# An encoder layer on one core: TensorE and the DMA queue of the mixer in source order

## The chip, the cores and the metric

The kernel runs on one core of a Trainium2 chip. The metric is device time of one execution in microseconds, lower is better. The kernel before took 881.35 us (median of three runs, 881.19 to 881.5). A core has TensorE (PE in the profile: matmuls and transposes, with PEld for its weight loads), VectorE (DVE), ScalarE (ACT), GpSimd (POOL) and SyncE (SP, which here only starts DMA transfers). Each takes its instructions from its own queue, one after the other, and they meet at semaphores.

## The reference

One layer of an encoder: half a SwiGLU step, a mixer, another half SwiGLU step, a final norm. Sequence 512, width 1024, float32 throughout.

```python
x = x + 0.5 * swiglu(rms_norm(x, ffn1_norm), ffn1_w_gate, ffn1_w_up, ffn1_w_down)
h = rms_norm(x, mix_norm)
u = h @ w_in                        # 512 fourier | 8x64 q | 2x64 k | 2x64 v
f_out = fourier_mixer(u[..., :512], fnet_w, fnet_b)
a_out = gqa_attention(u[..., 512:1024], u[..., 1024:1152], u[..., 1152:], q_norm, k_norm)
x = x + jnp.concatenate([f_out, a_out], axis=-1) @ w_out
x = x + 0.5 * swiglu(rms_norm(x, ffn2_norm), ffn2_w_gate, ffn2_w_up, ffn2_w_down)
return rms_norm(x, final_norm)
```

The Fourier half takes, for each of four groups of 128 channels, the real part of a two-dimensional Fourier transform over positions and channels, and then a 128 by 128 linear map. The attention half has eight query heads on two key/value heads; queries and keys get an RMS norm and a rotary turn in two axes, and the softmax is over all 512 positions.

## The kernel before

Every product is made of three passes: each operand is split into a high part, rounded to PE's fast float32 format, and a low part, the remainder. `product` (L100 to L103) issues high by high (L101), high by low (L102) and low by high (L103). So each weight block is loaded as it is (`raw_tile`, L85 to L87, a ring of three buffers), cast to its high part by ACT (L96; by VectorE at L94 for the two blocks f0 and f1), and its low part is made by VectorE (`lows`, L72). The parts stand in slots that are handed round; a slot is free when the last matmul that reads it is done.

The two FFNs (`ffn`) are recorded under `in_order()`: in them PE and SP keep the order of the source. The mixer between them is not. There a scheduler, at build time, orders the instructions of all engines by its own estimate of their times. The source order of the mixer is only its starting point.

The mixer, in the order of its source: k, the first query block q0 and v are projected (`project`; eight steps of one `product` each). `rope` turns k and q: it makes the squares for the norm (sq), a copy with the halves swapped (sw), and three VectorE steps with the tables cos and sin. For q1 to q3 the swap is made by four DMA transfers on SP's queue out of a copy (own). `heads` (pq, sc) sums the squares on PE, and VectorE, GpSimd (a power) and VectorE again turn them into a factor. `keys` (kp) transposes the factors of the keys (kw) and scales k with them; `value_stacks` (vp) transposes v.

Then the loop `attend` runs over 32 scores (t: query block, b: head group, c: block of 128 queries). At step n it issues the score n (s, L777 and L778; then mx on VectorE: a maximum, L781, and its scaling, L782; then the exponent e on ACT, L784), the transpose of the probabilities of step n - 4 (pt, L790; cast to ph on ACT, low part pl on VectorE), and the product with the values of step n - 6 (o, L809 and L810). A transpose of block kc reads all four exponents of its group, so the first of a group follows the group's last score at a distance of one step. Between the steps, in shares of a cost, stand the entries of the list `fill`: the projections q1 to q3, the Fourier half's projection (`fproject`, f, from the weight blocks f0 to f3), the fold of its linear map (`fold`, map), the transform over positions (`positions`, dft) and over channels (`channels`, pc and psn). After the loop come eight blocks of the output projection (out), each of eight products, four with the Fourier half (mh, ml) and four with attention (qa, qb), and the second FFN.

Loads stand where the cast of their block stands: `project` and `fload` call `weights`, which issues the load and the cast. cos and sin are loaded at the top of the mixer; the transform's tables chan, pos and odd come by GpSimd's queue.

Of the kernel before, what the change touches and what calls it, by code (L numbers as in the profile page):

```python
# [13 lines left out]
P = 128  # L14
S = 512
D = 1024
KD = D // P
# [7 lines left out]
FILL_LEAD = 0.1  # L25
# [18 lines left out]
def encoder(ctx, tc, A, out):  # L44
    nc = tc.nc
# [7 lines left out]
    def bank(name):  # L53
        return pp.tile([P, S], F32, tag="bank", name=name)
# [9 lines left out]
    def in_order():  # L64
        return tc.manual_schedule(engines={mybir.EngineType.PE, mybir.EngineType.SP})

    def run(steps):
        for _, f, a in steps:
            f(*a)
# [12 lines left out]
    def weight_slots():  # L82
        return (slot().rearrange("p (a b) -> p a b", b=P) for _ in range(2))

    def raw_tile(src, name, n=KD):  # L85
        raw = wp.tile([P, KD, P], F32, tag="raw", name=f"raw_{name}")
        nc.sync.dma_start(out=raw[:, :n, :], in_=src)  # L87
        return raw

    def weights(src, name, n=KD, raw=None):  # L90
        raw = raw or raw_tile(src, name, n)
        hi, lo = weight_slots()
        if name in HI_DVE:
            nc.vector.tensor_copy(hi[:, :n, :], raw[:, :n, :])  # L94
        else:
            nc.scalar.copy(hi[:, :n, :], raw[:, :n, :])  # L96
        lows(lo[:, :n, :], raw[:, :n, :], hi[:, :n, :])
        return hi, lo

    def product(ps, whi, wlo, mhi, mlo, first, last):  # L100
        nc.tensor.matmul(ps, whi, mhi, start=first, stop=False)  # L101
        nc.tensor.matmul(ps, whi, mlo, start=False, stop=False)  # L102
        nc.tensor.matmul(ps, wlo, mhi, start=False, stop=last)  # L103

    class Norm:
# [29 lines left out]
        def add(self, k):  # L135
            self.scale(k)
            self.sums(k)
# [360 lines left out]
    raws = [wp.tile([P, 4, 2, P], F32, tag="raw", name=f"raw_first{i}") for i in range(KH)]  # L498
# [45 lines left out]


    n2 = Norm(2)
    with tc.tile_pool(name="mix", bufs=1) as mp, tc.tile_pool(name="mixt", bufs=1) as mt:

        more = mp.tile([P, 2, KD * P], F32R, name="more")
        more = [more[:, i, :] for i in range(2)]  # L550
# [3 lines left out]
            return mt.tile([P, S], F32, tag="t", bufs=9, name=name)  # L554

        cos = mp.tile([P, S], F32, name="cos")
        nc.sync.dma_start(out=cos, in_=A["cos"])
        sin = mp.tile([P, S], F32, name="sin")
        nc.sync.dma_start(out=sin, in_=A["sin"])
        chan = mp.tile([P, 4, P], F32R, name="chan")  # L560
        pos = mp.tile([P, 2, 2, 514], F32R, name="pos")
        odd = mp.tile([1, 258], F32R, name="odd")

        sc = mp.tile([P, 4, 10], F32, name="sc")

        def project(c, name):

            whi, wlo = weights(A["wins"][c], f"in{c}")
            ps = bank(name)
            banks[name] = ps  # L570

            def step(k):
                product(ps, whi[:, k, :], wlo[:, k, :], hh[k], hl[k], k == 0, k == KD - 1)

            return [(0.65, step, (k,)) for k in range(KD)]
# [100 lines left out]
        fws = {}  # L676

        def fload(i):
            if i == "fw":
                fws[i] = [  # L680
                    w[:, :4, :].rearrange("p a b -> p (a b)")
                    for w in weights(A["fw"].rearrange("p (a b) -> p a b", b=P), "fw", 4)
                ]
                return
            src = A["winf"][i].rearrange("p a (b c) -> p (a b) c", c=P)
            if i == 3 and i not in fws:
                fws[i] = raw_tile(src, "f3")
                return
            h, l = weights(src, f"f{i}", raw=fws.get(i))
            fws[i] = [w.rearrange("p (a b) c -> p a (b c)", a=4) for w in (h, l)]  # L690

        def fproject(h, c, i):
# [25 lines left out]
        mh, ml = ([e[g // 2][g % 2].rearrange("p a b -> p (a b)") for g in range(4)] for e in (eh, el))  # L718
# [68 lines left out]
        def turn(t, b, kc):  # L787
            pt = bank(f"pt{t}{b}{kc}")
            for c in range(4):
                nc.tensor.transpose(pt[:, c * P : (c + 1) * P], prob[t, b, c][:, kc * P : (kc + 1) * P], ident)  # L790
            ph = mt.tile([P, S], F32R, tag="ph", bufs=3, name=f"ph{t}{b}{kc}")
            pl = mt.tile([P, S], F32R, tag="pl", bufs=3, name=f"pl{t}{b}{kc}")
            nc.scalar.copy(ph, pt)
            lows(pl, pt, ph)
            parts[t, b, kc] = ph, pl
            if b == 1 and kc == 0:

                zw = tp.tile([P, 4, 2, HD], F32, tag="wide", bufs=1, name=f"zw{t}")
                nc.vector.reciprocal(zs[t], zs[t])
                nc.gpsimd.tensor_copy(zw, zs[t].unsqueeze(3).to_broadcast([P, 4, 2, HD]))  # L800
                zs[t] = zw

        def values(t, b, kc):
            if kc == 0:
                outs[t, b] = bank(f"o{t}{b}")
            po = outs[t, b]
            ph, pl = parts[t, b, kc]
            w = vst[:, b, kc].rearrange("p a e -> p (a e)")
            nc.tensor.matmul(po, w, ph, start=kc == 0, stop=False)  # L809
            nc.tensor.matmul(po, w, pl, start=False, stop=kc == 3)  # L810
            if kc == 3:
                own = slice(b * HD, (b + 1) * HD)
                if b == 0:
                    pair[t] = tp.tile([P, S], F32, tag="u", name=f"oo{t}")
                o = pair[t]
                nc.scalar.copy(o[own], po[HD:P])
                nc.vector.tensor_tensor(out=o[own], in0=po[0:HD], in1=o[own], op=ALU.add)
                if b == 1:
                    zp = bank(f"zp{t}")
                    for c in range(4):  # L820
                        nc.tensor.transpose(
                            zp[:, c * P : (c + 1) * P], zs[t][:, c].rearrange("p a b -> p (a b)"), ident
                        )
                    nc.vector.tensor_tensor(out=o, in0=zp, in1=o, op=ALU.mult)
                    nc.scalar.copy(qa[t], o)
                    lows(qb[t], o, qa[t])


        scale = HD**-0.5
        key = project(0, "k")  # L830
        q0 = project(1, "q0")
        run(key)
        rope("k", qkg[:, 1:2])
        n1.column([n1.acc])
        val = project(5, "v")
        run(q0[:5])
        key_scales()
        run(q0[5:])
# [1 line left out]
        query(0)  # L840
        for t, n in ((chan, "chan"), (pos, "pos"), (odd, "odd")):
            nc.gpsimd.dma_start(out=t, in_=A[n])
        q1 = project(2, "q1")
        run(val[:2])
        keys()
# [12 lines left out]
        fill = []  # L858
# [4 lines left out]
        for t in (1, 2, 3):  # L863
            for k in range(KD):
                add(step, t, k, cost=0.65)
                if k == 0 and t < 3:
                    add(load, t + 1)
                if t == 3 and k in (0, 4):
                    add(fload, k // 4)
                if k == 3:  # L870
                    add(*((value_stacks,) if t == 1 else (heads, f"q{t - 1}", t, scale)), cost=0.3)
            add(query, t)
        for h in range(2):
            for n, c in enumerate((0, 2, 1, 3)):
                for i in range(2):
                    add(fproject, h, c, i, cost=1.3)
                    if h == 0 and n == 3 and i == 0:
                        add(fload, 3)
                if h == 0 and n == 0:
                    add(heads, "q3", 4, scale)  # L880
                if h == 0 and n in (1, 2):
                    add(fload, n + 1)
                if h == 1 and n == 0:
                    add(fload, "fw")
        add(fold, cost=1.3)
# [7 lines left out]
        def attend(n):  # L893
            def at(m):
                return m // 8, m // 4 % 2, m % 4

            if n < 32:
                scores(*at(n))
            if 4 <= n < 36:
                turn(*at(n - 4))  # L900
            if n >= 6:
                values(*at(n - 6))

        whole = sum(c for c, _, _ in fill)
        done = 0.0
        for n in range(38):
            while fill and done < whole * (FILL_LEAD + (1 - FILL_LEAD) * n / 38):
                done += fill[0][0]
                run([fill.pop(0)])
            attend(n)  # L910
        run(fill)

        mh, ml = mh + [qa[t] for t in range(4)], ml + [qb[t] for t in range(4)]
        for d in range(KD):
            whi, wlo = weights(A["wo"][d], f"o{d}")
            ps = bank(f"out{d}")
            for k in range(KD):
                product(ps, whi[:, k, :], wlo[:, k, :], mh[k], ml[k], k == 0, k == KD - 1)
            nc.vector.tensor_tensor(out=x[d], in0=ps, in1=x[d], op=ALU.add)
            n2.add(d)  # L920

# [5 lines left out]
    ready = (3, 4, 5)  # L927
# [158 lines left out]
```

## Time and profile before

| what | value |
|---|---|
| median of three runs | 881.35 us (881.19 to 881.5) |
| the profiled execution | 882.0 us |
| its span, from the first to the last instruction | 880.1 us |
| first FFN on PE, to the last down projection | to 353.2 us |
| mixer on PE | 353.2 to 523.6 us |
| granted clock of PE | 1.00 in the mixer, 0.995 over the span |
| DMA in the span | 85.55 MB, mean 97 GB/s |

The profile describes one execution. Its times are counted from the span's start. A row of the kind "L72 DVE ... pl<-pt,ph" names the source line, the engine, and what is written from what; lines are often those of a helper. A row of waits names who waited for whom, then the sum in us, the number of waits and the longest. A row of a timeline has the start and the length in us; what stands in brackets is the idle time of the engine before it and what ended that. A row of stretches has, for PE, PEld, DVE, ACT and POOL in turn, the busy time and the number of instructions, then PE's clock, the busy share of the DMA engines and GB/s. A DMA queue's row has packets, MB and the share of 16 DMA engines that its packets took. Busy time of PE is pipelined: a matmul's shown end is modelled and lies after the start of the next one.

### The profile page before, as it was taken

What the parts mean: (1) busy time and instruction counts of PE and PEld (TensorE: products, weight loads), DVE (VectorE), ACT (ScalarE), POOL (GpSimd) and SP (SyncE); (2) the same over time, 40 slices, a digit from 0 to 9 for tenths busy, and PEclk for the clock granted to TensorE, in tenths of its full rate; (3) what the DMA queues carried; (4) which work ended last, traced back from release to release, by engine and by line L of the source; (5) the groups of instructions that cost most, each with busy time, mean ns of one, the idle gap of its engine ahead of it and who ended that gap; (6) DMA issues with size and microseconds to landing.
All of it is one profiled execution on the core that took longest, in us unless ns stands there. A gap on an engine that the chain in (4) does not pass through costs nothing.

```text
span 880.1 us, 13432 instructions
## 1 busy us (share of the span) xinstructions
PE 863.1 (98%) x5334; PEld 766.7 (87%) x5334; DVE 640.4 (73%) x1003; ACT 451.0 (51%) x746; POOL 24.7 (3%) x32
## 2 busy tenths in 40 slices
PE   8999999999999999999999999999999999999995
PEld 5888999889989988888888888889998999889985
DVE  7798788459757837699888558977975688469444
ACT  7454466226525634677775436535652365327432
POOL 0000000000000000211000000000000000000002
PEclk9999999999999999999999999999999999999998
DMA  7324232333243113521110223242224232322212
GB/s 245 112 67 164 98 118 86 99 116 104 69 141 114 55 36 108 204 83 37 50 48 25 94 67 127 75 141 97 108 79 140 88 119 69 105 110 85 73 36 96
DMA packets 29150, 85.55 MB, mean 97 GB/s; under 512 B 3488, under 2 KB 6560, under 8 KB 28960
## 3 DMA queue, kind: packets, MB, share of 16 engines
q1 hardware_dynamic: 28560, 83.37, 28.1%
q0 software_dynamic: 384, 1.32, 0.5%
q8 instruction: 41, 0.67, 0.3%
q14 instruction: 21, 0.17, 0.1%
q10 hardware_dynamic: 144, 0.02, 0.0%
HBM read 81.81 MB, written 2.10 MB: 95 GB/s over the span
## 4 chain that ended last, share of the span: by engine, by line
PE 56%; issue 39%; DVE 2%; ACT 2%; DMA 1%; POOL 0%; SPq 0%; POOLq 0%; ACTq 0%; DVEq 0%
PE r L304 10%; PE q L304 5%; PE dn L103 4%; PE dn L101 4%; PE dn L102 4%; PE p L304 3%; PE gu L103 2%; PE gu L102 2%; PE gu L101 2%; PE out L101 2%; PE out L103 2%; PE out L102 2%; PE pt L790 1%; PE q L101 1%; PE q L102 1%
## 5 line engine op out<-in xcount | busy, mean ns | idle before, releaser
L304 PE MATMUL r<-rt,ring 128*128 128x256 f32 x1584 | 207.2, 283 | 0.0
L304 PEld LDWEIGHTS r<-rt,ring 128*128 128x128 f32 x1584 | 196.1, 188 | 2.4
L101 PE MATMUL dn<-at,ring 128*128 128x512 f32 x324 | 128.0, 395 | 0.8 <-ACT ring L96 0.8
L103 PE MATMUL dn<-at,ring 128*128 128x512 f32 x324 | 127.9, 395 | 0.3 <-DVE ring L72 0.3
L102 PE MATMUL dn<-at,ring 128*128 128x512 f32 x324 | 127.9, 395 | 0.0
L390 DVE SCALAR_TENSOR_TENSOR xt<-dn,xt 128x512 f32<-128x512 f32 x62 | 42.8, 690 | 89.4 <-PE dn L103 89.4
L304 PE MATMUL q<-rt,ring 128*128 128x256 f32 x792 | 104.8, 282 | 0.0
L96 ACT CAST ring<-raw_dn 128x768 fp32r<-128x768 f32 (+3 forms) x64 | 48.1, 754 | 108.2 <-PE dn L102 89.8
L304 PEld LDWEIGHTS q<-rt,ring 128*128 128x128 f32 x792 | 98.7, 188 | 0.0
L72 DVE TENSOR_TENSOR ring<-s,ring 128x1024 fp32r<-128x1024 f32 x66 | 80.3, 1220 | 16.7 <-PE r L304 9.7
L265 ACT CAST ring<-s 128x1024 fp32r<-128x1024 f32 x66 | 69.3, 1050 | 37.4 <-PE r L304 19.2
L103 PEld LDWEIGHTS dn<-at,ring 128*128 128x128 f32 x324 | 61.0, 188 | 15.2 <-DVE ring L72 0.7
L101 PEld LDWEIGHTS dn<-at,ring 128*128 128x128 f32 x324 | 60.9, 188 | 14.8 <-ACT ring L96 1.0
L102 PEld LDWEIGHTS dn<-at,ring 128*128 128x128 f32 x324 | 60.9, 188 | 13.9
L72 DVE TENSOR_TENSOR ring<-raw_dn,ring 128x768 fp32r<-128x768 f32 (+3 forms) x64 | 54.5, 854 | 11.3 <-ACT ring L96 8.9
L304 PE MATMUL p<-rt,ring 128*128 128x256 f32 x396 | 52.4, 282 | 0.0
L72 DVE TENSOR_TENSOR ring<-raw_g,ring 128x1024 fp32r<-128x1024 f32 x33 | 40.4, 1223 | 15.5 <-PE p L304 10.9
L304 PEld LDWEIGHTS p<-rt,ring 128*128 128x128 f32 x396 | 49.3, 188 | 0.0
L265 ACT CAST ring<-raw_g 128x1024 fp32r<-128x1024 f32 x33 | 34.6, 1049 | 22.9 <-PE r L304 9.9
L101 PE MATMUL gu<-ring 128*128 128x512 f32 x112 | 44.1, 394 | 0.9 <-ACT ring L527 0.9
L102 PE MATMUL gu<-ring 128*128 128x512 f32 x112 | 43.9, 392 | 0.0
L103 PE MATMUL gu<-ring 128*128 128x512 f32 x104 | 41.1, 395 | 0.8 <-DVE ring L72 0.7
(308 smaller groups left out, 1514.0 us busy)
## 6 DMA issues: line engine op xcount, KB each, us to landing
raw_g<-in_wgu SPq DMA_DIRECT2D x33, 512.0 KB, 3.7
raw_u<-in_wgu SPq DMA_DIRECT2D x33, 512.0 KB, 4.3
raw_dn<-in_wd SPq DMA_DIRECT2D x40, 384.0 KB, 3.0
raw_gu<-in_wgu SPq DMA_DIRECT2D x16, 512.0 KB, 3.6
raw_o<-in_wo SPq DMA_DIRECT2D x8, 512.0 KB, 3.5
raw_in<-in_wins SPq DMA_DIRECT2D x6, 512.0 KB, 4.1
raw_dn<-in_wd SPq DMA_DIRECT2D x8, 320.0 KB, 2.9
raw_dn<-in_wd SPq DMA_DIRECT2D x8, 256.0 KB, 2.6
```

What stands on the lines that cost most here:

```text
L72: nc.vector.tensor_tensor(out=lo, in0=src, in1=asf(hi), op=ALU.subtract)
L96: nc.scalar.copy(hi[:, :n, :], raw[:, :n, :])
L101: nc.tensor.matmul(ps, whi, mhi, start=first, stop=False)
L102: nc.tensor.matmul(ps, whi, mlo, start=False, stop=False)
L103: nc.tensor.matmul(ps, wlo, mhi, start=False, stop=last)
L265: nc.scalar.copy(hi, src)
L304: nc.tensor.matmul(ps, a[:, ks], b[:, i], start=first and i == 0 and o == 0, stop=i == KH - 1 and o == 2, skip_group_check=not first,)
L390: nc.vector.scalar_tensor_tensor(out=x[d][:, t], in0=ps[:, t], scalar=0.5, in1=x[d][:, t], op0=ALU.mult, op1=ALU.add)
L790: nc.tensor.transpose(pt[:, c * P : (c + 1) * P], prob[t, b, c][:, kc * P : (kc + 1) * P], ident)
```

## The change

The mixer too is recorded under `in_order()`: PE and SP keep the order of its source; the other engines are still ordered by the scheduler. With that come four edits of the source order. Loads are taken out of `weights` into a function `fetch`, called at places of their own: in0, in1 ahead of everything, in5 behind the calls for k and q0, then cos and sin, then in2; in3 behind the tables of the transform; in4, f0, f1 at the third step of q1, q2, q3, f2 at the seventh step of q3, and f3 and fw among the Fourier projections. Transposes stand five steps behind their scores instead of four, and the products with the values seven instead of six, so the loop has 39 steps instead of 38. f2 is cast one entry of the list earlier. And the eight products of an output block are issued in the order 0, 1, 2, 4, 5, 6, 3, 7.

SP's queue in the mixer was, in the order of its entries: in0, in1, in5, in2, cos, sin, in3, in4, f0, f1, f2, the four swaps of q1, f3, the swaps of q2, fw, the swaps of q3, and the blocks of w_out. It becomes: in0, in1, in5, cos, sin, in2, in3, in4, the swaps of q1, f0, the swaps of q2, f1, f2, the swaps of q3, f3, fw, and the blocks of w_out.

```diff
-    with tc.tile_pool(name="mix", bufs=1) as mp, tc.tile_pool(name="mixt", bufs=1) as mt:
+    with in_order(), tc.tile_pool(name="mix", bufs=1) as mp, tc.tile_pool(name="mixt", bufs=1) as mt:
...
+        raws = {}
+
+        def fetch(c):
+
+            if isinstance(c, int):
+                raws[c] = raw_tile(A["wins"][c], f"in{c}")
+            elif c == "fw":
+                raws[c] = raw_tile(A["fw"].rearrange("p (a b) -> p a b", b=P), c, 4)
+            else:
+                raws[c] = raw_tile(A["winf"][int(c[1])].rearrange("p a (b c) -> p (a b) c", c=P), c)
+
         def project(c, name):
 
-            whi, wlo = weights(A["wins"][c], f"in{c}")
+            whi, wlo = weights(None, f"in{c}", raw=raws[c])
...
         scale = HD**-0.5
+        fetch(0)
+        fetch(1)
         key = project(0, "k")
         q0 = project(1, "q0")
+        fetch(5)
+        nc.sync.dma_start(out=cos, in_=A["cos"])
+        nc.sync.dma_start(out=sin, in_=A["sin"])
         run(key)
         rope("k", qkg[:, 1:2])
         n1.column([n1.acc])
         val = project(5, "v")
+        fetch(2)
         run(q0[:5])
...
+        fetch(3)
         q1 = project(2, "q1")
         run(val[:2])
         keys()
...
+                if k == 2:
+                    add(fetch, (4, "f0", "f1")[t - 1])
                 if t == 3 and k in (0, 4):
                     add(fload, k // 4)
+                if t == 3 and k == 6:
+                    add(fetch, "f2")
...
                     if h == 0 and n == 3 and i == 0:
                         add(fload, 3)
+                        add(fetch, "fw")
                 if h == 0 and n == 0:
                     add(heads, "q3", 4, scale)
-                if h == 0 and n in (1, 2):
-                    add(fload, n + 1)
+                    add(fetch, "f3")
+                if h == 0 and n == 1:
+                    add(fload, 2)
...
             if n < 32:
                 scores(*at(n))
-            if 4 <= n < 36:
-                turn(*at(n - 4))
-            if n >= 6:
-                values(*at(n - 6))
+            if 5 <= n < 37:
+                turn(*at(n - 5))
+            if n >= 7:
+                values(*at(n - 7))
...
-        for n in range(38):
-            while fill and done < whole * (FILL_LEAD + (1 - FILL_LEAD) * n / 38):
+        for n in range(39):
+            while fill and done < whole * (FILL_LEAD + (1 - FILL_LEAD) * n / 39):
...
+        ready = 0, 1, 2, 4, 5, 6, 3, 7
         for d in range(KD):
             whi, wlo = weights(A["wo"][d], f"o{d}")
             ps = bank(f"out{d}")
-            for k in range(KD):
-                product(ps, whi[:, k, :], wlo[:, k, :], mh[k], ml[k], k == 0, k == KD - 1)
+            for k in ready:
+                product(ps, whi[:, k, :], wlo[:, k, :], mh[k], ml[k], k == ready[0], k == ready[-1])
```

More of the change, by code (lines that the diff above doesn't have):

```diff
@@ L556, in encoder @@
         cos = mp.tile([P, S], F32, name="cos")
-        nc.sync.dma_start(out=cos, in_=A["cos"])
         sin = mp.tile([P, S], F32, name="sin")
-        nc.sync.dma_start(out=sin, in_=A["sin"])
         chan = mp.tile([P, 4, P], F32R, name="chan")
@@ L679, in fload @@
             if i == "fw":
[L680 to L683, printed above, removed]
+                fws[i] = [w[:, :4, :].rearrange("p a b -> p (a b)") for w in weights(None, i, 4, raws[i])]
                 return
[L685 to L689, printed above, removed]
+            h, l = weights(None, f"f{i}", raw=raws[f"f{i}"])
             fws[i] = [w.rearrange("p (a b) c -> p a (b c)", a=4) for w in (h, l)]
```

## The prediction, made before the changed kernel ran

> **What bounds the kernel now.** I read the shares first, then the waits of TensorE (PE), then the stretches of the mixer (353 to 524 us; the two FFNs around it are not touched), and last the timelines of VectorE (DVE) and of SP, the queue that starts the loads. The columns of the stretches are the stretch, its length and each engine's busy time.
>
> ```profile
> PE 863.1 (98%) x5334; PEld 766.7 (87%) x5334; DVE 640.4 (73%) x1003; ACT 451.0 (51%) x746; POOL 24.7 (3%) x32
> ...
> PE o L809 <- ACT ph L793: 1.4, 2, 0.9
> PE f L700 <- ACT e L784: 1.3, 1, 1.3
> PE s L777 <- ACT e L784: 0.5, 1, 0.5
> PE pt L790 <- ACT e L784: 0.4, 1, 0.4
> ...
> 372.00:411.00 39.00, 37.75 (x215) 31.93 (x214) 37.84 (x79) 29.50 (x57) 5.52 (x4) 1.00 0.23 69
> 411.00:430.00 19.00, 19.00 (x138) 17.57 (x138) 15.27 (x36) 14.50 (x30) 2.25 (x2) 1.00 0.01 2
> ```
>
> PE bounds the mixer, and little is left to win: the four rows of waits are all that it waits there, 3.6 us. A matmul's shown end lies past the point at which the next could start (0.39 us against 0.23 for 512 columns), so I take each hole from start to start:
>
> ```profile
> 402.25 0.49 PE L809 MATMUL o<-ph,vst 128*128 128x512 f32 x1
> 403.99 0.38 PE L700 MATMUL f<-ring 128*128 128x256 f32 x1 [1.25 <-ACT e L784]
> ```
>
> 403.99 - 402.25 - 0.23 = 1.51 us lost. The same subtraction gives 1.16 at 437.5 us, 0.66 at 458.6, 0.56 at 466.3 and 0.70 at 471.0: 4.6 us in all, one of them early and 3.1 us late. That is the most that any order of PE can win here. The first hole has DVE behind it, which is busy 37.84 of 39 us from 372 to 411: there the mixer is bound by DVE as much as by PE.
>
> **Part 1: the work itself, 0.** The built program of the changed kernel has the same number of instructions on every engine. Loads, steps and order move, nothing is added. Transposes that the scheduler had split stand together again. After transposes a 512-column matmul takes 0.32 instead of 0.23 us to its successor (400.52 to 400.84 us), but the last transpose only 0.03 instead of 0.11, so fewer splits are worth nothing either.
>
> **Part 2: the key transpose, 1.6 us lost.** In source order kp (L644) follows two steps of v; before, it followed all eight.
>
> ```profile
> 366.95 1.23 DVE L72 TENSOR_TENSOR ring<-raw_in,ring 128x1024 fp32r<-128x1024 f32 x1 [0.84 <-ACT ring L96]
> 368.09 0.16 DVE L618 SCALAR_TENSOR_TENSOR sc<-sc,r 128x8 f32<-128x8 f32 x1
> 368.36 0.43 DVE L638 COPY kw<-sc 128x512 f32<-128x512 f32 x1
> ```
>
> PE starts v at 366.26 as before; six matmuls at 0.233 bring it to 367.66. kw is there at 368.36 + 0.43 = 368.79, since in DVE's new order it still stands behind the low part of in3, whose cast waits for q0's last matmul (365.9). PE waits 1.2 us, and behind kp the whole mixer waits. That is the lower bound.
>
> The upper bound comes from SP's queue. in2 was started at 351.30 us, ahead of cos and sin; now it stands behind them, and they wait for the last matmul of the FFN:
>
> ```profile
> 351.30 0.33 SPq L87 DMA_DIRECT2D raw_in<-in_wins  x1
> 353.36 0.33 SPq L557 DMA_DIRECT2D cos<-in_cos  x1
> 353.74 0.43 SPq L559 DMA_DIRECT2D sin<-in_sin  x1
> 355.52 1.46 SPq L87 DMA_DIRECT2D raw_in<-in_wins  x2
> 361.01 14.12 SPq L87 DMA_DIRECT2D raw_f<-in_winf  x3
> 381.40 2.48 SPq L591 DMA_DIRECT2D sw_q<-own_q  x4
> ...
> q0 software_dynamic: 113, 0.77, 99.1%
> ```
>
> So in2 starts at 354.2. Its cast ran at 358.68, held by k's weight slots. With the fastest landing of such a load (3.5 us) it is there at 357.7 and nothing changes. But the last line above is the only queue that moved anything from 357.0 to 359.5 us: POOL's 1 MB of pos, while in3, started by SP at 355.52, stood still. If in2 stands still too, its 0.52 MB lands at about 361.2 (from 359.6 at 0.33 MB/us, the mean of 359.5 to 365). The cast (1.05), sq_k (0.54) and four sw_k (2.6) end at 365.4, the three rotary steps of DVE (2.0) at 367.4, the first sc steps at 367.8; POOL's power (1.64) ends at 369.5, and kw at 370.3: a wait of 2.7 us. I take 1.6, nearer the lower end, since in2 is in the queue 1.3 us before in3 and both queues moved data from 356 to 357.
>
> [...]
>
> **Part 3: f0 comes late, 2.2 us lost.** The words say "well ahead"; SP's new order says the opposite for f0. Its load stood ahead of q1's four swaps and was started at 361.0, 18.7 us before its cast. Now it follows the swaps. q1 ends on PE at about 381.0 (before 379.2, plus 1.2 of part 2, plus the first score's 0.46), sq_q and own_q end at 382.3, four swaps take 2.48, f0 starts at 384.85 and lands 3.6 later (median of these loads): 388.4. The last swap lands at 386.35 (4.0 after the first one's start, as before), and DVE is free for f0's cast at 387.85. Queued behind that cast in DVE are the maxima of s010 and of all later scores. What f0 leaves open:
>
> ```profile
> 379.66 0.68 DVE L94 CAST ring<-raw_f 128x1024 fp32r<-128x1024 f32 x1
> 380.26 0.42 DVE L72 TENSOR_TENSOR vst<-vp,vst 128x256 fp32r<-128x256 f32 x1
> 380.60 1.22 DVE L72 TENSOR_TENSOR ring<-raw_f,ring 128x1024 fp32r<-128x1024 f32 x1
> ```
>
> These 1.9 us were done before the first maximum; now DVE stands idle for scores between 380 and 388, and does f0 in the stretch where it is the bound. From f0's cast to the scaled maximum of s103 DVE has 45 instructions (28 of 0.7, 14 of 0.16, 3 of 1.2 us; each next one starts 0.08 before the end of the last): 21.4 us. Back to back that ends at 387.85 + 21.4 = 409.3; at DVE's pace of before (26.2 us of 382.41 to 408.95 for 24.4 of such a sum, 1.07) from 388.4 at 411.3. The exponent e103 (0.78, and 0.1 of hand-over) ends at 410.1 or 412.2. PE gets to the transpose of e103 after 184 matmuls of 512 (0.231), 24 of 256 (0.119), 47 transposes (0.109) and 5 sums (0.81): 54.5 us after 353.2, plus 1.2: 408.9. It waits 1.2 to 3.3 us; I take the middle, 2.2. It stands in the place of the early hole of 1.51.
>
> **Part 4: five steps, 1.0 us left of 3.1.** The late holes came from an order in which o (L809) followed its transpose directly (436 us) or a transpose its exponent. In the new order two steps of about 2.7 us lie between a transpose and its o, against 0.59 + 0.68 us of casts, and one more step between a score and its transpose. Where DVE keeps up, these holes are gone. From s303 to s313 it doesn't: 10.5 us of DVE at pace 1.07 are 11.2, against 9.9 of PE (21 of 512, 24 of 256, 20 transposes). It falls 1.3 us back, where e311 and the maximum of s312 stand behind three weight casts of w_out. I take two waits of 0.5. Bounds: 0, and the 3.1 of before.
>
> **Part 5: the end, 0.** Before, three output blocks were interleaved and hid the last channels. Now out0 starts alone, in the order 0, 1, 2, 4, 5, 6, 3, 7. Between the last matmul of psn2 and the first use of el10 lie 3.2 us of PE; the chain (0.37 fq, two of 0.40 for fo, 0.62 cast, 0.69 low part, and 0.7 of the other pair's work on DVE) is 3.2 too. Without that cover it would cost 0.5. POOL's queue has the same order.
>
> **Sum.** 1.6 + 2.2 + 1.0 = 4.8 us lost against 4.6 before: +0.2. The profiled execution took 882.0 (span 880.1, and 1.9 around it), 0.65 over the median of the runs; on the median the forecast is 881.35 + 0.2 = 881.5 us. It is a change of nothing: gain late, loss early.
>
> **The rivals.** *DVE keeps up (faster).* The bounds' low ends: 1.2 + 1.2 + 0 = 2.4, so 881.35 - 2.2 = 879.1 us. For it: DVE has only 15.27 of 19 us after 411, and PE no other wait. Against it: 37.84 of 39 before that. With kp hidden too, nothing is below 881.35 - 4.6 = 876.8.
> *The loads starve DVE (slower).* in2 lands at 361 and f0 at 388.4 with DVE at its old pace: 2.7 + 3.3 + 1.0 = 7.0, so 881.35 + 2.4 = 883.8 us; with the late holes of before as well 9.1, 885.9. It decides if PE's two waits at kp and at the transpose of e103 pass 5.4 us together. For it: the empty queue of 357 to 359.5. Against it: in2 is needed first at 358.7.
>
> **The numbers.** About 0.2% (1.8 us) is what a measurement can tell from no change. Forecast 0.40 (its own range 879.6 to 883.1), faster rival 0.32, slower rival 0.28. The range that leaves one in ten on each side: 877.8 to 885.3.
>
> **What would show it.** Right: PE waits for kw before kp, 1 to 3 us; f0's cast starts after 387 us and DVE is idle between 380 and 388; one wait of PE for an exponent near 410; no wait of o for ph after 430. Wrong: no wait at kp (part 2), f0's cast not waiting for its load (part 3), waits of o for ph (part 4), or PE holes in the mixer under 2.5 or over 7 us in sum.

## The result, and the profile after

| | before | after |
|---|---|---|
| median of six runs each | 881.43 us (881.19 to 882.0) | 888.38 us (885.92 to 893.21) |
| ratio, 95% interval | 1 | 1.0082 (1.0066 to 1.0098) |
| profiled execution, its span | 882.0, 880.1 us | 888.36, 886.5 us |
| first matmul of k to last of out, start to start | 170.15 us | 175.94 us |

The change costs 0.8%, and 5.8 of the 6.4 us by which the span grew lie between the first matmul of k and the last one of the output projection, over the same 946 rows of matmuls. First the page's busy times and TensorE's waits in the mixer (sum, number, longest):

```profile
PE 866.8 (98%) x5334; PEld 769.5 (87%) x5334; DVE 640.7 (72%) x1003; ACT 452.3 (51%) x746; POOL 26.8 (3%) x32
...
PE kp L653 <- DVE kw L647: 3.5, 1, 3.5
PE pt L792 <- ACT e L786: 2.0, 2, 1.8
PE dft L101 <- DVE pl L72: 0.9, 1, 0.9
PE pq_k L616 <- ACT sq_k L592: 0.4, 1, 0.4
PE out L102 <- DVE el L72: 0.3, 1, 0.3
```

Every wait of o for ph is gone, and others have come, three of them early: kp for kw, an exponent, and pq_k. Start to start, as holes are counted in the prediction, these three are 3.67, 2.00 and 0.60 us; dft loses 1.02 and out 0.51. Next the chain of waits that ends in kp (start, length, what):

```profile
354.64 7.58 DMA raw_in<-in_wins
...
362.31 1.05 ACT ring L96
...
363.88 0.68 ACT sw_k L602
...
366.67 0.75 DVE rot_k L607
...
369.11 2.59 POOL sc L624
...
371.99 0.44 DVE kw L647
372.43 0.04 issue
372.48 1.11 PE kp L653 x4
```

in2 takes 7.58 us to land. Its cast then holds up all that ACT has queued behind it: the square that pq_k waits for, and the four sw_k that the rotary steps wait for. GpSimd's power takes another 2.6 us. Then the stretches (length; busy time of PE, PEld, DVE, ACT, POOL; clock of PE, share of the DMA engines, GB/s):

```profile
353.20:372.00 18.80, 15.33 (x77) 12.30 (x75) 9.71 (x17) 12.35 (x17) 5.31 (x5) 1.00 0.49 182
372.00:411.00 39.00, 38.47 (x194) 31.64 (x194) 32.84 (x67) 25.21 (x48) 4.31 (x3) 0.96 0.17 55
411.00:430.00 19.00, 17.16 (x122) 15.45 (x122) 17.64 (x41) 13.54 (x30) 5.38 (x3) 1.00 0.25 84
430.00:450.00 20.00, 20.00 (x142) 18.14 (x142) 17.12 (x35) 14.80 (x30) 0.62 (x1) 1.00 0.14 54
```

DVE does 32.84 us of work from 372 to 411 where it did 37.84, and is busier from 411 to 430 (17.64 for 15.27), where the exponent is late. The clock's 0.96 stands for something that the profile of before does not have, as narrower stretches show:

```profile
368.90:372.00 3.10, 0.07 (x1) 0.00 (x0) 1.47 (x4) 3.04 (x5) 2.58 (x1) 1.00 0.00 0
372.00:375.40 3.40, 2.92 (x9) 2.54 (x10) 2.19 (x4) 1.03 (x3) 0.00 (x0) 0.51 0.01 2
375.40:377.00 1.60, 1.60 (x11) 1.35 (x11) 1.55 (x4) 1.45 (x3) 0.00 (x0) 0.98 0.00 0
```

TensorE stands idle for 3.5 us, and from 0.4 us before the end of that wait its granted clock is halved for 3.4 us: the multiplies of v start 0.43 us apart and not 0.233. 3.0 us of the halved stretch lie behind the wait, and half of them, about 1.5 us, is lost.

### The profile page after: what moved, and what is told of

Its sections match the earlier page's. It is cut to its first block, busy times and chain, and to the rows that moved or that the text cites. A ratio compares the mean times of both kernels' runs of the same rounds, so it can differ in the third digit from the quotient of the medians.

```text
span 886.5 us, 13424 instructions
## 1 busy us (share of the span) xinstructions
PE 866.8 (98%) x5334; PEld 769.5 (87%) x5334; DVE 640.7 (72%) x1003; ACT 452.3 (51%) x746; POOL 26.8 (3%) x32
## 4 chain that ended last, share of the span: by engine, by line
PE 52%; issue 39%; DVE 5%; DMA 2%; ACT 1%; POOL 1%; SPq 0%; POOLq 0%; ACTq 0%; DVEq 0%
PE r L304 10%; PE q L304 5%; PE dn L103 4%; PE dn L102 4%; PE dn L101 4%; PE gu L101 3%; PE p L304 3%; PE gu L102 3%; PE gu L103 3%; PE out L102 2%; PE out L103 2%; PE out L101 2%; PE pt L792 1%; DMA raw_in<-in_wins 1%; DVE mx L783 1%
## 5 line engine op out<-in xcount | busy, mean ns | idle before, releaser
L101 PE MATMUL gu<-ring 128*128 128x512 f32 x112 | 44.9, 401 | 0.7 <-ACT ring L527 0.7
L102 PE MATMUL gu<-ring 128*128 128x512 f32 x112 | 44.7, 399 | 0.0
L103 PE MATMUL gu<-ring 128*128 128x512 f32 x104 | 41.5, 399 | 0.0
```

## The experiments

Where no other base is named, each is the changed kernel with the edit shown, run against the kernel before on the same chip. Most undo one late step of the change each; the last ones of the list take these apart.

**in2 ahead of cos and sin again.**

```diff
         fetch(5)
+        fetch(2)
         nc.sync.dma_start(out=cos, in_=A["cos"])
...
         val = project(5, "v")
-        fetch(2)
```

> The changed kernel with one load moved back: in2 is started ahead of cos and sin, where it stood before the change. Theory (the late load of in2 starves VectorE: it lands at 362.2 instead of 354.8, and the wait of kp is 3.5 us instead of 1.2): in2 lands before 358, kp waits 0.8 to 1.5 us, PE's clock stays at 1.00 from 372 to 376 us, and the time is 882.5 to 885 us. Rival (kp waits because source order puts it after two steps of v, whenever in2 lands): kp still waits over 3 us and the time stays at 887 to 889.

Measured: 884.99 us (883.97 to 886.84), ratio 1.0039 (1.0027 to 1.0051). Against the change's 888.38 us the late landing of in2 is half of the loss; against the second measurement of the change, 886.25 us (further down), it is 1.3 us, under a third. TensorE's waits, and the stretches around the exponent's wait:

```profile
PE pt L792 <- ACT e L786: 1.8, 1, 1.8
PE kp L653 <- DVE kw L647: 0.9, 1, 0.9
```

```profile
410.30:412.20 1.90, 0.08 (x2) 0.07 (x2) 1.90 (x7) 0.99 (x3) 0.00 (x0) 1.00 0.90 353
412.20:413.90 1.70, 1.70 (x14) 1.61 (x15) 1.47 (x4) 1.68 (x5) 0.00 (x0) 1.00 0.80 290
413.90:417.40 3.50, 3.50 (x17) 3.20 (x16) 2.29 (x7) 1.43 (x3) 1.38 (x1) 0.51 0.01 4
```

pq_k no longer waits, and kp loses 1.10 us start to start. The clock stays whole behind kp, but is halved 1.9 us after the wait for the exponent had ended.

**The key transposes behind all of v.**

```diff
-        run(val[:2])
+        run(val)
         keys()
-        run(val[2:5])
         heads("q0", 1, scale)
-        run(val[5:])
         scaled_values()
```

> The changed kernel with kp and the sums for q0 issued after all eight steps of v instead of after two, in2 still late. Theory (only the place of the wait in PE's queue makes the late load cost time): 18 matmuls of 0.233 us, 4.2 us, now stand ahead of kp, kw comes at about 372.0 as in the changed kernel, kp waits under 0.3 us, the clock stays at 1.00, and the time is 882 to 884.5 us. Rival (the late VectorE work is needed soon anyway, by qa0 and the first scores): the wait moves to the first score and under 1.5 us is won, 887 or more.

Measured: 885.44 us (882.45 to 886.18), ratio 1.0038 (1.0026 to 1.005), some 1 us above what was expected. kp waits no more and the clock stays whole in the profiled execution, but in2 is still late: pq_k loses 1.0 us, one o waits 1.1 us for its low part, and the exponents cost 2.5 us.

**f0, f1 and f2 early.**

```diff
-                if k == 2:
-                    add(fetch, (4, "f0", "f1")[t - 1])
+                if k == 2 and t < 3:
+                    add(fetch, (4, "f2")[t - 1])
+                if t == 1 and k in (4, 6):
+                    add(fetch, "f0" if k == 4 else "f1")
...
-                if t == 3 and k == 6:
-                    add(fetch, "f2")
```

> The changed kernel with f0 and f1 started ahead of q1's swaps and f2 ahead of q2's, nothing else. Theory (f0's cast waits for its load and holds the maxima behind it, part 3 of the prediction): VectorE is not idle before f0's cast, the wait of the transpose for e103 (2.0 us in the changed kernel) falls under 0.8 us, and the time is 1 to 2.5 us less than the changed kernel's. Rival (VectorE is the bound of that stretch whenever f0 lands): the wait stays above 1.5 us and the time within 0.7 us of the changed kernel's.

Measured: 885.09 us (883.08 to 886.43), ratio 1.0036 (1.0024 to 1.0048): 3.3 us under 888.38, more than expected, and 1.2 under the 886.25 of the second measurement, as expected. The exponent's wait falls from 2.0 to 0.2 us. In the changed kernel, f0's start in SyncE's queue and its cast on DVE were:

```profile
389.87 0.53 SPq L87 DMA_DIRECT2D raw_f<-in_winf  x1
```

```profile
393.71 0.69 DVE L94 CAST ring<-raw_f 128x1024 fp32r<-128x1024 f32 x1 [0.89 <-DMA raw_f<-in_winf]
```

Here f0 is started at 363.07, with f1 behind it, and cast 9.4 us sooner, where DVE had stood idle between maxima:

```profile
384.28 0.68 DVE L94 CAST ring<-raw_f 128x1024 fp32r<-128x1024 f32 x1
```

kp still waits 2.9 us, and the clock is halved from 370.3 to 373.7 us, from shortly before the wait ends.

**All three edits together.**

> All three edits together: in2 ahead of cos and sin, kp after all of v, f0 and f1 ahead of the swaps. If the three waits and the clock make up the loss, 877.5 to 880.5 us, faster than the kernel before, with holes of PE in the mixer under 2.5 us. If order on PE and SP is itself worse than the scheduler's here, 882 us or more.

Measured: 878.61 us (878.36 to 879.27), ratio 0.9966 (0.9955 to 0.9978): faster than both kernels. All the waits that TensorE has left in the mixer, and two stretches:

```profile
PE dft L101 <- DVE pl L72: 0.9, 1, 0.9
PE out L102 <- DVE el L72: 0.3, 1, 0.3
```

```profile
372.00:411.00 39.00, 39.00 (x226) 33.42 (x224) 38.01 (x84) 30.93 (x62) 6.02 (x4) 1.00 0.19 58
411.00:430.00 19.00, 19.00 (x136) 17.23 (x135) 17.25 (x37) 13.73 (x28) 2.75 (x2) 1.00 0.15 54
```

The 170.15 us of before are 167.23. Alone, each edit took between 2.9 and 3.4 us off the change's 888.38; together 9.8. Against the second measurement of the change, 886.25, the same medians are 0.8 to 1.3 and 7.6 us lower, so the time that one edit alone is worth is known only to some 2 us. That its wait goes is in the traces; its worth in time is better read from the next three kernels.

**One of the three left out.** The next three kernels are this one, each with one edit undone.

> The kernel of 878.61 us with the key transposes back in the place that the change gave them, behind two steps of v: in2 ahead of cos and sin and f0, f1, f2 early are left. Theory: kp waits 0.9 to 1.1 us for kw, as with in2 ahead alone, and nothing else comes back; a wait of 1 us is rarely followed by a halved clock; median 879.3 to 880.3 us. Rival (the 1 us is taken from a later wait): within 0.3 us of 878.6.

> The kernel of 878.61 us with in2 back behind cos and sin: key transposes behind v and f0, f1, f2 early are left. Theory: pq_k waits 0.8 to 1.3 us, since ACT squares k behind the cast of the late in2, kp doesn't wait, and one o near 386 us waits 1.1 us as with the key transposes alone; in part of the runs the clock is halved for 3.4 us behind these waits (1.7 us each); median 880.5 to 883.5 us. Rival (behind v nothing of the lateness reaches TensorE): 878.6 to 879.5 us.

> The kernel of 878.61 us with f0, f1 and f2 back in the place that the change gave them: in2 ahead and key transposes behind v are left. Theory: the wait of 2 us for the exponent e103 near 412 us is back, and in part of the runs a halved clock behind it (1.7 us): median 880.5 to 883 us. Rival (with DVE and ACT undisturbed ahead of 380 us the late cast of f0 is caught up): 878.6 to 879.5 us.

| undone | median us | ratio to before | what comes back |
|---|---|---|---|
| key transposes behind v | 879.86 (879.24 to 881.84) | 0.9983 (0.9974 to 0.9992) | kp for kw 0.9 us |
| in2 ahead | 881.79 (880.18 to 884.31) | 1.0002 (0.9994 to 1.0011) | pq_k for sq_k 1.7 us, halved clock at 366.5 us |
| f0, f1, f2 early | 883.42 (882.28 to 885.32) | 1.0024 (1.0013 to 1.0034) | pt for e 1.8 us, halved clock at 413 us |

The wait forecast for one o near 386 us did not come back without in2, the wait for sq_k was longer than the 0.8 to 1.3 us expected, and the late f0's median lies 0.4 us above its range; the rest came as the theories had it. The late f0 costs most (4.8 us of median): 2.0 us start to start at its wait, and 1.7 us by the halved clock in the profiled execution.

**Why in2 lands so late.** The first attempt moved GpSimd's three loads in the source only:

```diff
-        for t, n in ((chan, "chan"), (pos, "pos"), (odd, "odd")):
-            nc.gpsimd.dma_start(out=t, in_=A[n])
         fetch(3)
...
         scaled_values()
+        for t, n in ((chan, "chan"), (pos, "pos"), (odd, "odd")):
+            nc.gpsimd.dma_start(out=t, in_=A[n])
```

> The changed kernel with GpSimd's three loads (chan, pos and odd, 1.28 MB, first used 80 us later) moved from behind query(0) to behind scaled_values(), so that they are issued after key_scales. Nothing else is moved; in2 stays behind cos and sin in SyncE's queue. Theory (in2 is late because these loads share the rings with it): in2, issued at 354.6 us, lands near 358.5 us and not at 362.2, the wait of kp for kw falls from 3.5 to at most 1.2 us, the clock stays at 1.00, and the median is 884.0 to 886.0 us, with the waits for exponents near 415 us left. Rival (in2 is late because of its place behind cos and sin in SyncE's own queue): in2 lands after 361 us, the wait stays above 2.5 us and the median stays above 887 us.

GpSimd's order is the scheduler's, and it issued the loads where it had: the instructions of every engine stood in the changed kernel's order. So this run asked nothing; it is a second measurement of the change: 886.25 us (883.36 to 888.16), ratio 1.005 (1.0036 to 1.0065), 2.1 us under the first. In its profile kp waits only 1.0 us, since a wait of 1.2 us for pq_k and a halved clock from 365.4 us had made TensorE late before: kp starts at 372.00 where it started at 372.48. The second attempt made the same move and put GpSimd's queue under the source's order too:

```diff
-    with in_order(), tc.tile_pool(name="mix", bufs=1) as mp, tc.tile_pool(name="mixt", bufs=1) as mt:
+    pool_too = {mybir.EngineType.PE, mybir.EngineType.SP, mybir.EngineType.Pool}
+    with tc.manual_schedule(engines=pool_too), tc.tile_pool(name="mix", bufs=1) as mp, tc.tile_pool(name="mixt", bufs=1) as mt:
```

> The changed kernel with GpSimd's own queue in the source's order too in the mixer, and its three loads (chan, pos, odd, 1.28 MB) behind scaled_values(), so that they are issued behind the pow of k and of q0, after 370 us. In the run called e9_pos_late GpSimd had issued them at 354 us all the same, and that program was the changed kernel's. in2 stays behind cos and sin. Theory (in2 is late because these loads share the rings with it): in2, issued at 354.6 us, lands before 359.5 us and not at 362.2, TensorE waits neither for pq_k nor more than 1.2 us for kw, and the median is 884 to 886 us, with the wait for an exponent near 415 us and in part of the runs a halved clock behind it left. Rival (its place behind cos and sin is enough to make it late): in2 lands after 361 us, pq_k and kw are waited for as before, and the median lies between 886.3 and 888.4 us.

Measured: 884.95 us (883.8 to 886.11), ratio 1.0039 (1.0026 to 1.0051). The DMA queues (packets, MB, share of the engines) from 357.0 to 359.5 us, first in the changed kernel, then here; and here the cast of in2:

```profile
q1 hardware_dynamic: 133, 0.48, 52.3%
q0 software_dynamic: 84, 0.45, 50.0%
```

```profile
q1 hardware_dynamic: 241, 0.88, 95.5%
```

```profile
359.56 1.05 ACT L96 CAST ring<-raw_in 128x1024 fp32r<-128x1024 f32 x1 [3.08 <-DMA raw_in<-in_wins]
```

With the engines to itself, SyncE's queue moves 0.88 for 0.48 MB, and in2 is cast at 359.56 and not at 362.31. pq_k waits no more and kp 0.9 us. So it takes both: the place behind cos and sin, and the loads beside it. No view shows the rings that the two theories name; the rows show shares of the DMA engines. The median is not that of the loads alone, since from 386 us on DVE and ACT also have another order here than in the changed kernel.

**The halved clock by itself.**

```diff
             kp = bank("kp")
+            for _ in range(15):
+                nc.tensor.matmul(kp, hh[0][:, :P], hh[0], start=True, stop=True)
```

> The changed kernel with fifteen extra 128x512 multiplies into the bank kp, whose result the transposes then overwrite, placed before the four transposes that wait for kw: they fill the 3.9 us for which TensorE stood idle (15 x 0.233 = 3.5 us) and wait for nothing themselves. Theory (the idle time halves the granted clock, and the 1.4 us behind it are the price of that): kp comes at the same time, about 372.5 us, but its transposes and the multiplies of v behind it run at full clock, 0.233 us from start to start and not 0.45; the clock shows 1.00 from 372 to 376; median 886.0 to 887.5 us, and the spread of the runs is smaller than 885.9 to 893.2. Rival (the slow multiplies behind the wait have another cause, such as the operands or the loads that land): the multiplies stay at 0.45 us and the median stays at 888 to 889.5 us.

Measured: 888.46 us (885.35 to 889.56), ratio 1.007 (1.0058 to 1.0083): the median expected did not come. Around the wait for pq_k and kp:

```profile
363.00:364.30 1.30, 0.18 (x2) 0.09 (x1) 0.61 (x1) 1.27 (x3) 0.00 (x0) 1.00 0.53 217
364.30:366.00 1.70, 1.70 (x12) 1.57 (x13) 0.96 (x2) 1.68 (x3) 0.00 (x0) 1.00 0.02 10
366.00:369.40 3.40, 3.40 (x12) 2.71 (x11) 2.39 (x7) 2.14 (x4) 0.00 (x0) 0.50 0.00 0
369.40:374.00 4.60, 4.60 (x22) 3.73 (x21) 2.97 (x5) 3.75 (x6) 2.58 (x1) 1.00 0.01 2
```

At kp the clock is whole, as the theory had it, and the multiplies behind it start 0.23 us apart. But in this execution the clock had been halved earlier, from 366.0, behind the 1.1 us wait for pq_k. That made TensorE late, and the fifteen multiplies pushed kp to 374.18 us, past kw (372.7). So the run shows that the slow multiplies do not belong to their place, but not what the median would be without them.

**Four steps instead of five**, in the kernel with all three edits: the loop of the diff with its old distances, 4 and 6, and 38 steps.

> The kernel with in2 ahead of cos and sin, the key transposes behind v and f0, f1, f2 early (878.61 us), with probabilities turned four steps behind their scores and values six steps behind, as before the change. Theory (the fifth step is what keeps TensorE from waiting for exponents and for ph): waits of pt for e and of o for ph or pl come back, 1 to 3 us in sum, and the median is 879.5 to 881.5 us. Rival (source order alone gives the cover, the fifth step adds none): median within 0.4 us of 878.6.

Measured: 885.46 us (883.7 to 888.25), ratio 1.0044 (1.0032 to 1.0056), and of the waits:

```profile
PE pt L792 <- ACT e L786: 4.6, 5, 1.7
```

In source order the fifth step is worth 6.9 us. The direction was expected, not the size: the profiled execution, the fastest of the six, shows 4.6 us of waits for exponents where the kernel with all three edits has none in its list. o still waits for no ph.

**The natural order of the output products**, in the same kernel: `ready = tuple(range(KD))`.

> The kernel with in2 ahead of cos and sin, the key transposes behind v and f0, f1, f2 early (878.61 us), with the output projection's products in their natural order 0 to 7 instead of 0, 1, 2, 4, 5, 6, 3, 7. Theory (the reordering covers the last Fourier group's low half): out0 waits for that low half at its fourth product and stops 0.5 to 1.5 us longer than now, median 879.1 to 880.1 us. Rival (the last heads' values, product 7, end last anyway): the wait only moves, median within 0.3 us of 878.6.

Measured: 880.46 us (879.92 to 883.2), ratio 0.9989 (0.998 to 0.9998). The output blocks wait 0.7 us for a high half and 0.6 for low halves, where they waited 0.3. The reordering is worth 1.9 us, a little more than expected.

## Why the prediction was right and wrong

The direction of its slower rival came true, by its own test and by the two loads that it named, though not with in2 standing still as it had it: the waits at kp and at the transpose of e103 were to pass 5.4 us together, and they were 3.67 + 2.00 = 5.67. The time was not its 883.8 but 888.38. By the prediction's steps:

- *Part 2, the key transpose* (1.6, bounds 1.2 to 2.7) is the step that failed. It measured 3.67 at kp, and 0.60 at pq_k ahead of it, for which there was no term. "I take 1.6, nearer the lower end" was the choice of an in2 that lands almost in time. It landed at 362.2, 1.0 us past even the starved case's 361.2. The chain counted from there held, but for the power of GpSimd: 2.58 us and not 1.64. The lower bound is 1.13 us by its own numbers (368.79 - 367.66), and with in2 ahead kp did lose 1.10.
- Its reasoning weighed two cases, in2 starved or in2 in time. Neither came: from 357.0 to 359.5 us both queues moved data (0.48 and 0.45 MB), and in2 was late all the same. A share of the engines, 52.3% for SyncE's queue, was not enough for it. From 359.5 to 361.5 us the two queues of the changed kernel moved:

```profile
q0 software_dynamic: 68, 0.56, 71.2%
q1 hardware_dynamic: 60, 0.23, 33.3%
```

The packets are nearly equal in number (68 and 60), but one of GpSimd's carries some 8 KB and one of SyncE's some 4 KB, so SyncE's queue, in which in2 stood, got 0.23 of 0.79 MB. From 357.0 to 359.5 us the kernel of before had 99.1% for GpSimd's queue alone, and the kernel with in2 ahead has 95.6% for it against 6.7%; what decides between these patterns was not shown.
- *A term was missing*: the halved clock behind a wait, about 1.5 us in the profiled execution. In before no hole passed 1.51 us and the clock was 1.00 throughout the mixer, so its profile gave no warning.
- *Part 3, f0* (2.2, bounds 1.2 to 3.3) held: 2.00 at e103, and 0.30 at an o. f0 was started 5.0 us later than worked out (389.87 for 384.85), mostly since TensorE's delays ahead of it were 3.67 + 0.60 + 1.5 = 5.8 us and not 1.2, and DVE cast it at 393.71. The wait came out as forecast because TensorE was late by about as much as f0. DVE was not idle throughout 380 to 388, but in gaps of up to 1.0 us.
- *Part 4, five steps* (1.0 left) held: 1.02 at dft and 0.32 at a transpose, and no o waits for ph after 430 us. That four steps would have cost so much in this order was not seen.
- *Part 5, the end* (0): 0.51 us at out0, the price that it gave without cover. The cover of 3.2 us against a chain of 3.2 was no cover.
- *Part 1* (0) can stand: without its holes the stretch of before is 170.15 - 4.6 = 165.6 us, and that of the kernel with all three edits 167.23 - 1.85 = 165.4.

Sum: 4.27 + 2.30 + 1.34 + 0.51 = 8.4 us lost where 4.8 were forecast, and more than the 7 us that the prediction had named as a sign of being wrong. With the clock's 1.5 it is about 9.9, against 4.6 before. That gives +5.3, and the trace +5.8 for the stretch; the other 0.5 us is not accounted for. The range ended at 885.3, since its ends held no second cost behind a wait.

## What to carry to other kernels

A load that is moved in its queue is costed by when its last byte lands beside all that is in flight then, and everything that its consumer's engine has queued behind it pays, too: here a place two entries further back cost 3.2 us (881.79 for 878.61), with GpSimd's loads beside it. An order in which the heaviest engine runs without gaps was fragile here: behind some of the waits of 1.1 to 3.5 us the clock was halved for 3.4 us, so count a second cost there (1.4 to 1.7 us in these profiles). And a good pattern can hide behind a bad detail: source order, the fifth step and the order of the output products were together worth 3.0 us over before (ratio 0.9966), once four loads and the key transposes stood elsewhere. The fifth step is needed for it: with four steps the same kernel is 3.7 us slower than before (ratio 1.0044).

## What the runs showed of the hardware

**A halved clock behind short waits.** In nine stretches of the mixer, over eight profiled executions, the granted clock was 0.50 for 3.4 us, 1.4 to 1.7 us lost each time (an estimate: half of what lies behind the wait). A wait of 1.1 to 3.5 us stood ahead of each, at kp, at pq_k or at an exponent; in the two longest, at kp, the drop came 0.4 and 0.6 us before the wait ended, in the others 1.0 to 2.1 us after it, while TensorE was busy. The wait of 1.8 us for an exponent had no such stretch behind it in the change's own profile and in two others, and had one in three. The wait of 1.3 us for an exponent in before had none, nor had the longest wait with four steps, 1.7 us. So the length of a wait alone does not tell whether the clock drops; what else decides was not shown.

For every execution the mean granted clock is on record: 0.990 to 0.993 in the six of the change (0.990 in the slowest, 893.21 us), 0.991 to 0.995 in its second measurement (0.995 in the fastest, 883.36 us), 0.995 or 0.996 with all three edits. From 0.992 to 0.9956, the means of the first and the last, is about 3 us (an estimate: 0.0036 of 888 us). So the clock probably costs the median of the change more than the one stretch of its profile, and makes a part of the spread of its runs. Since the mean also holds the start and the end of the span, the number of halved stretches in each execution is not shown.

**GpSimd's power behind DVE.** The power of 128x8 in the keys' scales took 1.64 us in nine profiles and 2.58 to 2.63 in five. In all five DVE had begun the low part of in3 0.10 to 0.15 us before it, and the power ended 1.5 us after the end of that instruction; in the nine DVE began 0.49 to 1.50 us after the power. In the changed kernel, and in the second measurement of it:

```profile
369.11 2.58 POOL L624 TENSOR_TENSOR sc<-sc,mhalf 128x8 f32<-128x8 f32 x1 [7.82 <-DVE sc L623]
```

```profile
368.96 1.23 DVE L72 TENSOR_TENSOR ring<-raw_in,ring 128x1024 fp32r<-128x1024 f32 x1
```

```profile
369.58 1.64 POOL L624 TENSOR_TENSOR sc<-sc,mhalf 128x8 f32<-128x8 f32 x1 [8.60 <-DVE sc L623]
```

```profile
370.07 1.23 DVE L72 TENSOR_TENSOR ring<-raw_in,ring 128x1024 fp32r<-128x1024 f32 x1 [0.57 <-ACT ring L96]
```

The 0.94 us lie on the way to kw. What lengthens the power was not shown; the five profiles show only the order of the starts that goes with it. In the other order nothing grew longer: in the nine, DVE's instruction began before the power's shown end and took 1.23 us all the same.
